# Token rows of keys and values in a hybrid decoder step: 32x32 block transposes on VectorE in place of TensorE transposes

## The chip, the cores and the metric

One Trainium2 chip, one core of it. The metric is the device time of one execution in microseconds, as the median of the runs. A core has TensorE (matmuls, with a weight load beside each), VectorE, ScalarE and GpSimd for the elementwise work, and SP (SyncE), whose queue starts most DMA transfers. In the profile these are PE and PEld, DVE, ACT, POOL and SP.

## What is computed

One inference step of two layers of a decoder. The tokens are 16 meta tokens, 256 prompt tokens and 8 sample sequences of 8 tokens, 336 in all, each 2048 wide. A layer normalizes the tokens and projects them to eight pieces of 2048 columns. Four of these (q, k, v and a gate) feed the retention branch of 8 heads, the others a pooling branch and two gates. The part that matters here:

```
qh = rope(q); kh = rope(k) / 16; vh = v            # per head, 256 wide
scores = einsum('bihd,bjhd->bhij', q, k) * decay
intra  = einsum('bhij,bjhe->bihe', scores, v)
inter  = einsum('bihd,bhde->bihe', q, S) * q_decay
S_new  = S * exp(n * lg) + einsum('bjhd,bjhe->bhde', k * k_decay, v)
```

The prompt starts from an empty state and returns one state of 256x256 a head; each of the 8 sample sequences has its own state S of 256x256 a head, which is read, used and updated. Results are the outputs of both kinds of tokens, the pooling histories and all states.

## The kernel before

**Layout.** Activations are kept transposed: 128 channels in the partitions, tokens along the free dimension, so that a head's keys are one tile of [128, 2, 336] (two halves of 256 channels). All products are taken as three matmuls over a high and a low part of each operand: `hi_of` (L157) rounds on ScalarE to the high part, `lo_of` (L163) subtracts it on VectorE.

**The steps.** The weights of every projection are cut into steps of 512x256 (`steps`, filled by `job`, L89). A step is 24 matmuls (`main_step`, L195), which add up in one of two accumulators in PSUM; four steps make one block of 256 output channels. The main loop (L876) runs over all steps and does in step s, in this program order: the DMA of the weights of step s+4 on SP (`dma_step`), the split of the weights of step s+2 into high (ScalarE, L159) and low (VectorE, L165) parts (`split_step`), the main matmuls of step s, and then the events that are registered for step s. The schedule is written out by hand: each engine runs its instructions in this program order. The split's high and low tiles have four buffers, the raw weights five.

**A head** (`head`, L296) takes 16 steps: 4 for k, 4 for v, 4 for q, 4 for the gate `rg`. `at` (L86) registers a function for a step; in `head` `E(d, fn)` does so relative to the head's first step, and events with d of 16 and more fall into the steps of the next head. `ev_k`, `ev_v`, `ev_q`, `ev_rg` run behind the last step of each block and empty its accumulator; keys and queries are rotated there (`rope`, L301, four VectorE instructions).

**Token rows.** The state updates need keys and values with tokens in the partitions. `tok` (L321) makes them for token blocks of 128, 128 and 80: two TensorE transposes (L328) into a PSUM tile of `side()`, then the high part by ScalarE and the low part by VectorE, with the decay `kd` as scale for keys. This is 12 transposes a head for 16 heads (8 in each of two layers). `stack_out` (L332) writes the rows of block 2, where the sample tokens are, to DRAM on GpSimd's queue; `stack_in` (L338) reads them back on SP's queue in a stacked form: `kttail`, `vttail`, `kts` and `vbd`. With these `sdo(b)` (L425) updates the state of sample sequence b (two matmuls, one VectorE instruction, one DMA out), and `pstate` (L350) makes the prompt's state. `sload(b)` (L411) loads a state into one of 8 buffers on SP's queue; `inter` (L416) reads it before `sdo` updates it in place.

**Around it.** `scores2` (L389, step 14) needs the queries split by `split_q` (step 12); `pv(b)` (L470, steps 17, 19 and 24) multiplies the scores with the value rows and calls `norm`, `norm2` follows a step later, and `back` (L493, step 26) transposes the result on TensorE (L499) for the next projection. In the first head of layer 0 some events are `kl` = 3 steps later, since the norm of the input is not known earlier.

Of the kernel before, what the change touches and what calls it, by code (L numbers as in the profile page):

```python
# [6 lines left out]
F32 = mybir.dt.float32  # L7
F32R = mybir.dt.float32r
# [11 lines left out]
T = NP + NB * NS  # L20
HEADS = 8
HD = 256
# [10 lines left out]
NR0, NR1, NR2 = NP, NP - 128, T - 256  # L33
# [44 lines left out]
def build(tc, a, o, g8):  # L78
    nc = tc.nc
# [6 lines left out]
    def at(s, fn, *args):  # L86
        events[s].append(lambda: fn(*args))
# [15 lines left out]
    def open_pool(name, side=None, **kw):  # L103
        P[name] = tc.alloc_tile_pool(name=name, bufs=1, side=side, reuse_waits="tile", **kw)
        return P[name]
# [4 lines left out]
    def bc(ap, n=2):  # L110
        return ap.unsqueeze(1).to_broadcast([128, n, ap.shape[-1]])
# [9 lines left out]
    def side():  # L121
        return sidep.tile([128, 512], F32, tag="side", bufs=4, name="side")
# [16 lines left out]
    ident = cst[:, C_ID:C_ID + 128]  # L139
# [17 lines left out]
    def hi_of(out, in_, scale=None):  # L157
        if scale is None:
            nc.scalar.copy(out=out, in_=in_)  # L159
        else:  # L160
            nc.scalar.activation(out=out, in_=in_, func=ACTF.Copy, scale=scale)  # L161

    def lo_of(out, in_, hi, scale=None):  # L163
        if scale is None:
            nc.vector.tensor_tensor(out=out, in0=in_, in1=hi.bitcast(F32), op=ALU.subtract)  # L165
        else:
            nc.vector.scalar_tensor_tensor(out=out, in0=in_, scalar=scale, in1=hi.bitcast(F32),  # L167
                                           op0=ALU.mult, op1=ALU.subtract)
# [92 lines left out]
    H = {}  # L261

    for l in range(DEPTH):
# [10 lines left out]
        def z_of(acc, tile_, n):  # L274
            nc.vector.tensor_tensor(out=tile_[:, :, n], in0=acc[:, :, n], in1=bc(rstd[:, n]), op=ALU.mult)

        def open_r(l=l, a_side=a_side):
            p = open_pool("r", side=a_side)
            t = p.tile([128, 2, 8, 32], F32, name="qpad")
            nc.gpsimd.memset(t, 0.0)  # L280
            H["qpad"] = t
            t = p.tile([128, SC], F32, name="sc")
            nc.gpsimd.memset(t[64:128, NR0 + NR1:SC], 0.0)
            H["sc"] = t
            t = p.tile([128, 2, 4, HD], F32R, name="vbd")
            nc.gpsimd.memset(t.bitcast(F32), 0.0)
            H["vbd"] = t
            for key in ("kt", "vt"):
                t = p.tile([128, HD], F32R, name=key + "tail")
                nc.gpsimd.memset(t[64:128].bitcast(F32), 0.0)  # L290
                H[key + "tail"] = t

        def tmp():
            return P["r"].tile([128, 2, T], F32, tag="tmp", bufs=6, name="tmp")

        def head(h, l=l, c0=c0, n=n, nt=nt):  # L296
            hs = {}
            rp = lambda shape, dt, tag, bufs=1: P["r"].tile(shape, dt, tag=tag, bufs=bufs, name=tag)
            kd = lambda b, rows=128: cst[0:rows, C_KD + 3 * h + b:C_KD + 3 * h + b + 1]

            def rope(acc, out, n):  # L301
                t1, t2 = tmp(), tmp()
                nc.vector.tensor_tensor(out=t1[:, :, n], in0=acc[:, :, n], in1=bc(cosr[:, n]), op=ALU.mult)
                nc.vector.tensor_tensor(out=t2[:, :, n], in0=acc[:, :, n], in1=bc(sinr[:, n]), op=ALU.mult)
                nc.vector.tensor_tensor(out=out[:, 0, n], in0=t1[:, 0, n], in1=t2[:, 1, n], op=ALU.subtract)
                nc.vector.tensor_tensor(out=out[:, 1, n], in0=t1[:, 1, n], in1=t2[:, 0, n], op=ALU.add)

            def ev_k(acc):
                hs["kr"] = tmp()
                rope(acc, hs["kr"], slice(0, T))  # L310

            def split_k():
                hs["khi"], hs["klo"] = rp([128, 2, T], F32R, "khi"), rp([128, 2, T], F32R, "klo")
                hi_of(hs["khi"], hs["kr"])
                lo_of(hs["klo"], hs["kr"], hs["khi"])

            def ev_v(acc):
                hs["vr"] = tmp()
                z_of(acc, hs["vr"], slice(0, T))

            def tok(src, b, key, scale):  # L321
                rows = (128, 128, NR2)[b]
                if b == 2:
                    hs[key] = rp([128, 3, HD], F32R, key + "hi"), rp([128, 3, HD], F32R, key + "lo")
                hi, lo = hs[key]
                ps = side()
                for d in range(2):
                    nc.tensor.transpose(ps[:rows, 128 * d:128 * d + 128], hs[src][:, d, 128 * b:128 * b + rows], ident)  # L328
                hi_of(hi[:rows, b], ps[:rows, :HD], scale)
                lo_of(lo[:rows, b], ps[:rows, :HD], hi[:rows, b], scale)  # L330

            def stack_out(key):  # L332
                hs[key + "d"] = tc.dram_tile([NR2 // 8, 4, 8, HD], F32, name=key + "d")
# [159 lines left out]
            def back():  # L493
                ac = tmp()
                on = hs["on"]
                for d in range(2):
                    ps = side()
                    for b, (r0, rows) in enumerate(((c0, 128 - c0), (128, 128), (256, NR2))):
# [5 lines left out]
                                    in_=ac[:, :, n])  # L504

            b0, e = job(wblk(w_in, OFF["k"] + HD * h), 4, h_rhs, 0, ev_k, 3 if l == 0 and h == 0 else 0)
            job(wblk(w_in, OFF["v"] + HD * h), 4, h_rhs, 0, ev_v)
            job(wblk(w_in, OFF["q"] + HD * h), 4, h_rhs, c0, ev_q)
            job(wblk(w_in, OFF["rg"] + HD * h), 4, h_rhs, c0, ev_rg)
            E = lambda d, fn, *ar: at(b0 + d, lambda: fn(*ar))  # L510
            kl = 3 if l == 0 and h == 0 else 0
            E(4 + kl, split_k)
            E(6 + kl, tok, "kr", 2, "kt", kd(2, NR2))
            E(6 + kl, tok, "kr", 0, "kt", kd(0))
            E(7 + kl, tok, "kr", 1, "kt", kd(1))
            E(7 + kl, stack_out, "kt")
            E(9 + kl, stack_in, "kt")
            E(9 + kl, tok, "vr", 2, "vt", None)
            E(9 + kl, tok, "vr", 0, "vt", None)
            E(10 + kl, tok, "vr", 1, "vt", None)  # L520
            E(10 + kl, stack_out, "vt")
            E(12 + kl, stack_in, "vt")
            E(12, split_q)
            E(16, pstate)
            E(11, scores)
            E(14, scores2)
            for b in range(NB):
                E(6 + b, sload, b)
            E(15, inter)
            for b in range(NB):  # L530
                E(15 + b, sdo, b)
            E(16, inter_copy)
            E(17, pv, 0)
            E(18, norm2, 0)
# [8 lines left out]
        if l == 0:  # L543
            at(6, open_r)
        else:
            at(r0 - 1, open_r)
        for h in range(HEADS):
            head(h)
# [357 lines left out]
    parts = (xsq, H["sq_last"][:, 0], H["sq_last"][:, 1])  # L906
# [73 lines left out]
```

## Time and profile before

| What | Value |
|---|---|
| median of 3 runs | 2835.64 us (2835.21 to 2836.82) |
| the profiled execution | 2836.14 us |
| its span in the trace | 2834.4 us |
| mean granted TensorE clock | 0.997 of full speed |
| busy: TensorE, VectorE, ScalarE, GpSimd | 99%, 53%, 33%, 12% |
| moved by DMA | 516.64 MB, mean 182 GB/s |

A row of the profile names a line of the kernel (L328), an engine, an operation, the tiles out<-in, a shape as partitions x elements, and how often it occurs. Busy times are in us, means of one instruction in ns. In the timelines and the chain each row begins with its start in us from the start of the span and its length in us. The chain that ended last is followed back from the last instruction of the execution; time that an engine has in the chain is time on the path. Matmuls overlap, so the time of one in the chain is shorter than its listed duration.

### The profile page before, as it was taken

To read this page: it belongs to the slowest core of one execution; us is meant where nothing else is said; L and a number is where in the kernel's file an instruction comes from. 1 tells how busy PE (TensorE), PEld (TensorE's weight loads), DVE (VectorE), ACT (ScalarE), POOL (GpSimd) and SP (SyncE) were. 2 spreads that over 40 slices of the span, in tenths; PEclk is the share of its full clock that TensorE was granted. 3 is DMA by queue.
4 is the path that set the end of the run, shared out by engine and by line. 5 is a ranking of instruction groups with operands and counts; after the bars stand their busy time and mean duration, and the time that the engine had idled before them with its cause. 6 is when DMAs were issued, how large, how long until landed. Compare 5 with 4: busy or idle time off the path is not lost.

```text
span 2834.4 us, 46399 instructions
## 1 busy us (share of the span) xinstructions
PE 2819.7 (99%) x19234; PEld 2796.5 (99%) x19234; DVE 1509.9 (53%) x1906; ACT 936.2 (33%) x1121; POOL 341.3 (12%) x543
## 2 busy tenths in 40 slices
PE   9999999999999999999999999999999999999998
PEld 9999999999999999999999999999999999999998
DVE  6555555554345664345456666555544455644543
ACT  5333333334233333233333333333342333333333
POOL 1222222210000000000112222222100000000001
PEclk9999999999999999999999999999999999999998
DMA  7566565654544444444555666666555544444443
GB/s 262 208 211 208 208 206 195 227 188 165 164 161 153 147 147 136 152 173 167 180 184 209 211 211 211 216 219 215 205 168 176 171 153 160 142 158 163 172 162 129
DMA packets 174260, 516.64 MB, mean 182 GB/s; under 512 B 23888, under 2 KB 46672, under 8 KB 174032
## 3 DMA queue, kind: packets, MB, share of 16 engines
q1 hardware_dynamic: 151264, 448.37, 46.4%
q0 software_dynamic: 21696, 63.99, 6.4%
q8 instruction: 151, 2.47, 0.4%
q10 hardware_dynamic: 1088, 1.31, 0.1%
q14 instruction: 61, 0.50, 0.1%
HBM read 447.91 MB, written 66.57 MB: 182 GB/s over the span
## 4 chain that ended last, share of the span: by engine, by line
PE 99%; DVE 0%; DMA 0%; issue 0%; POOL 0%; SPq 0%; DVEq 0%; ACT 0%; ACTq 0%
PE acc L155 93%; PE side L155 6%; PE side L328 1%; PE side L499 0%; DMA raw<-in_w_in_dram 0%; DVE xf L922 0%; PE side L252 0%; POOL trs L913 0%; DVE whi L190 0%; DVEq L968 0%; DVE h_lo L167 0%; DVE xs L794 0%; ACT sq L799 0%; DVE wlo L165 0%; SPq L841 0%
## 5 line engine op out<-in xcount | busy, mean ns | idle before, releaser
L155 PE MATMUL acc<-act_hi,whi 128*128 128x320 f32 (+1 forms) x3328 | 1039.6, 312 | 0.0
L155 PE MATMUL acc<-act_lo,whi 128*128 128x320 f32 (+1 forms) x3328 | 1037.3, 312 | 0.0
L155 PE MATMUL acc<-act_hi,wlo 128*128 128x320 f32 (+1 forms) x3328 | 1036.2, 311 | 0.0
L165 DVE TENSOR_TENSOR wlo<-raw,whi 128x1024 fp32r<-128x1024 f32 (+1 forms) x721 | 865.5, 1220 | 293.3 <-ACT whi L159 285.4
L159 ACT CAST whi<-raw 128x1024 fp32r<-128x1024 f32 x719 | 733.8, 1049 | 499.6 <-PE acc L155 394.9
L155 PE MATMUL acc<-h_hi,whi 128*128 128x336 f32 x2304 | 731.6, 319 | 0.0
L155 PE MATMUL acc<-h_lo,whi 128*128 128x336 f32 x2304 | 727.6, 317 | 0.9 <-DVE h_lo L167 0.9
L155 PE MATMUL acc<-h_hi,wlo 128*128 128x336 f32 x2304 | 725.8, 317 | 0.0
L155 PEld LDWEIGHTS acc<-act_lo,whi 128*128 128x128 f32 x3328 | 626.5, 188 | 0.0
L155 PEld LDWEIGHTS acc<-act_hi,wlo 128*128 128x128 f32 x3328 | 625.1, 188 | 0.0
L155 PEld LDWEIGHTS acc<-act_hi,whi 128*128 128x128 f32 x3328 | 624.9, 188 | 0.0
L155 PEld LDWEIGHTS acc<-h_lo,whi 128*128 128x128 f32 x2304 | 435.3, 189 | 1.4 <-DVE h_lo L167 1.4
L155 PEld LDWEIGHTS acc<-h_hi,wlo 128*128 128x128 f32 x2304 | 432.8, 188 | 0.0
L155 PEld LDWEIGHTS acc<-h_hi,whi 128*128 128x128 f32 x2304 | 432.3, 188 | 0.3 <-issue 0.3
L432 DVE SCALAR_TENSOR_TENSOR sraw<-sraw,side 128x512 f32<-128x512 f32 x128 | 87.9, 687 | 175.4 <-PE side L155 175.4
L433 POOL DMA_DIRECT2D out_ret_s_dram<-sraw x128 | 71.6, 560 | 524.1 <-DVE sraw L432 518.0
L226 POOL TENSOR_TENSOR xsq<-sq 128x336 f32<-128x336 f32 (+1 forms) x2 | 1.8, 894 | 564.8 <-ACT sq L222 564.8
L161 ACT ACTIVATE kthi<-side,cst 128x256 fp32r<-128x256 f32 (+1 forms) x48 | 21.0, 470 | 136.4 <-PE side L328 136.4
L159 ACT CAST vthi<-side 128x256 fp32r<-128x256 f32 (+1 forms) x48 | 16.2, 372 | 146.1 <-PE side L328 146.1
L683 POOL DMA_DIRECT2D out_pool_u_dram<-uc x16 | 8.8, 547 | 440.4 <-DVE uc L638 440.4
L596 DVE SCALAR_TENSOR_TENSOR mb<-tr,acc 128x336 f32<-128x336 f32 (+1 forms) x32 | 14.4, 493 | 81.0 <-PE acc L155 81.0
L403 DVE TENSOR_TENSOR sc<-side,dtab 128x416 f32<-128x416 f32 (+1 forms) x16 | 9.3, 583 | 90.3 <-PE side L155 90.3
(165 smaller groups left out, 1844.0 us busy)
## 6 DMA issues: line engine op xcount, KB each, us to landing
raw<-in_w_in_dram SPq DMA_DIRECT2D x512, 512.0 KB, 4.3
sraw<-in_state_ret_dram SPq DMA_DIRECT2D x128, 256.0 KB, 4.2
out_ret_s_dram<-sraw POOLq DMA_DIRECT2D x128, 256.0 KB, 2.6
raw<-in_proj_ret_dram SPq DMA_DIRECT2D x64, 512.0 KB, 4.3
raw<-in_proj_pool_dram SPq DMA_DIRECT2D x64, 512.0 KB, 5.3
raw<-in_w_out_dram SPq DMA_DIRECT2D x64, 512.0 KB, 5.1
raw<-in_pool_w_dram SPq DMA_DIRECT2D x16, 512.0 KB, 3.3
kts<-ktd SPq DMA_DIRECT2D x16, 256.0 KB, 3.0
```

Of the source, the lines that this page charges most:

```text
L155: nc.tensor.matmul(out, lhsT, rhs, start=start, stop=stop)
L159: nc.scalar.copy(out=out, in_=in_)
L161: nc.scalar.activation(out=out, in_=in_, func=ACTF.Copy, scale=scale)
L165: nc.vector.tensor_tensor(out=out, in0=in_, in1=hi.bitcast(F32), op=ALU.subtract)
L226: eng.tensor_tensor(out=xsq[:, n], in0=sq[:, 0, n], in1=sq[:, 1, n], op=ALU.add)
L328: nc.tensor.transpose(ps[:rows, 128 * d:128 * d + 128], hs[src][:, d, 128 * b:128 * b + rows], ident)
L403: nc.vector.tensor_tensor(out=sc[:, w], in0=ps[:, w], in1=dtab[:, w], op=ALU.mult)
L432: nc.vector.scalar_tensor_tensor(out=s2, in0=s2, scalar=g8[h], in1=up, op0=ALU.mult, op1=ALU.add)
L433: nc.gpsimd.dma_start(out=o["ret_s"][l, b, h].rearrange("p (d e) -> p d e", d=2), in_=s)
L596: nc.vector.scalar_tensor_tensor(out=t[:, d, n], in0=H["tr", l, i][:, d, n], scalar=1.0, in1=acc[:, d, n], op0=ALU.add, op1=ALU.mult)
L683: nc.gpsimd.dma_start(out=o["pool_u"][l, 2 * g + i], in_=gs.pop(("uc", i)))
```

## The change

Keys and values are kept in fixed tiles of [128, 2, 384], `kr` and `vr`, whose columns behind the 336 tokens are zero. `turn` copies a tile to token rows in 32x32 blocks: for a group of 32 channels (`a_`, four of them) and a group `t` of 32 tokens in each block of 128, one VectorE transpose reads 32 partitions and writes 32 other partitions of a tile `tok` in SBUF; it covers both halves of the channels and all token blocks at once, 192 elements a partition (128 for t = 3, where block 2 has no tokens). Each event of `turn` has four of these instructions; keys have them in steps 5 to 8, values in steps 9 to 12. `tok` now takes its high and low parts from that tile. The steps of `tok`, `stack_out` and `stack_in` move, and `pstate` and `sdo` come two steps later.

```diff
--- before.py
+++ after.py
@@ -279,6 +279,10 @@
             t = p.tile([128, 2, 8, 32], F32, name="qpad")
             nc.gpsimd.memset(t, 0.0)
             H["qpad"] = t
+            for key in ("kr", "vr"):
+                t = p.tile([128, 2, 384], F32, name=key)
+                nc.gpsimd.memset(t[:, :, T:384], 0.0)
+                H[key] = t
             t = p.tile([128, SC], F32, name="sc")
             nc.gpsimd.memset(t[64:128, NR0 + NR1:SC], 0.0)
             H["sc"] = t
@@ -306,28 +310,36 @@
                 nc.vector.tensor_tensor(out=out[:, 1, n], in0=t1[:, 1, n], in1=t2[:, 0, n], op=ALU.add)
 
             def ev_k(acc):
-                hs["kr"] = tmp()
-                rope(acc, hs["kr"], slice(0, T))
+                rope(acc, H["kr"], slice(0, T))
 
             def split_k():
                 hs["khi"], hs["klo"] = rp([128, 2, T], F32R, "khi"), rp([128, 2, T], F32R, "klo")
-                hi_of(hs["khi"], hs["kr"])
-                lo_of(hs["klo"], hs["kr"], hs["khi"])
+                kr = H["kr"][:, :, 0:T]
+                hi_of(hs["khi"], kr)
+                lo_of(hs["klo"], kr, hs["khi"])
 
             def ev_v(acc):
-                hs["vr"] = tmp()
-                z_of(acc, hs["vr"], slice(0, T))
-
-            def tok(src, b, key, scale):
+                z_of(acc, H["vr"], slice(0, T))
+
+            def turn(key, parts):
+                src = H[key + "r"].rearrange("p d (b t i) -> p d b t i", b=3, t=4)
+                if 0 in parts:
+                    hs[key + "tok"] = rp([128, 3, HD], F32, "tok", 2)
+                dst = hs[key + "tok"].rearrange("p b (d a k) -> p d b a k", d=2, a=4)
+                for a_ in parts:
+                    q = slice(32 * a_, 32 * a_ + 32)
+                    for t in range(4):
+                        nb = 3 if t < 3 else 2
+                        nc.vector.transpose(dst[32 * t:32 * t + 32, :, 0:nb, a_], src[q, :, 0:nb, t])
+
+            def tok(b, key, scale):
                 rows = (128, 128, NR2)[b]
                 if b == 2:
-                    hs[key] = rp([128, 3, HD], F32R, key + "hi"), rp([128, 3, HD], F32R, key + "lo")
-                hi, lo = hs[key]
-                ps = side()
-                for d in range(2):
-                    nc.tensor.transpose(ps[:rows, 128 * d:128 * d + 128], hs[src][:, d, 128 * b:128 * b + rows], ident)
-                hi_of(hi[:rows, b], ps[:rows, :HD], scale)
-                lo_of(lo[:rows, b], ps[:rows, :HD], hi[:rows, b], scale)
+                    hs[key + "t"] = rp([128, 3, HD], F32R, key + "thi"), rp([128, 3, HD], F32R, key + "tlo")
+                hi, lo = hs[key + "t"]
+                raw = hs[key + "tok"][:rows, b]
+                hi_of(hi[:rows, b], raw, scale)
+                lo_of(lo[:rows, b], raw, hi[:rows, b], scale)
 
             def stack_out(key):
                 hs[key + "d"] = tc.dram_tile([NR2 // 8, 4, 8, HD], F32, name=key + "d")
@@ -510,25 +522,28 @@
             E = lambda d, fn, *ar: at(b0 + d, lambda: fn(*ar))
             kl = 3 if l == 0 and h == 0 else 0
             E(4 + kl, split_k)
-            E(6 + kl, tok, "kr", 2, "kt", kd(2, NR2))
-            E(6 + kl, tok, "kr", 0, "kt", kd(0))
-            E(7 + kl, tok, "kr", 1, "kt", kd(1))
-            E(7 + kl, stack_out, "kt")
-            E(9 + kl, stack_in, "kt")
-            E(9 + kl, tok, "vr", 2, "vt", None)
-            E(9 + kl, tok, "vr", 0, "vt", None)
-            E(10 + kl, tok, "vr", 1, "vt", None)
-            E(10 + kl, stack_out, "vt")
-            E(12 + kl, stack_in, "vt")
+            for i in range(4):
+                E(5 + i + kl, turn, "k", (i,))
+                E(min(9 + i + kl, 12), turn, "v", (i,))
+            E(9 + kl, tok, 2, "k", kd(2, NR2))
+            E(9 + kl, stack_out, "kt")
+            E(9 + kl, tok, 0, "k", kd(0))
+            E(10 + kl, tok, 1, "k", kd(1))
+            E(11 + kl, stack_in, "kt")
+            E(13, tok, 2, "v", None)
+            E(13, stack_out, "vt")
+            E(13, tok, 0, "v", None)
+            E(14, tok, 1, "v", None)
+            E(15, stack_in, "vt")
             E(12, split_q)
-            E(16, pstate)
+            E(18, pstate)
             E(11, scores)
             E(14, scores2)
             for b in range(NB):
                 E(6 + b, sload, b)
             E(15, inter)
             for b in range(NB):
-                E(15 + b, sdo, b)
+                E(17 + b, sdo, b)
             E(16, inter_copy)
             E(17, pv, 0)
             E(18, norm2, 0)
```

## Rows read from the trace of the kernel before

**Rows 1.** The page, part 1: busy us (share of the span) xinstructions.

```profile
PE 2819.7 (99%) x19234; PEld 2796.5 (99%) x19234; DVE 1509.9 (53%) x1906; ACT 936.2 (33%) x1121; POOL 341.3 (12%) x543
```

**Rows 2.** TensorE's waits, first and last of four; us in total, times, longest.

```profile
PE side L252 <- DVE sinr L250: 1.5, 1, 1.5
...
PE side L155 <- ACT sq L799: 0.6, 1, 0.6
```

**Rows 3.** The chain that ended last: start us, us, what; L328's pieces.

```profile
46.25 0.44 PE side L328 x4
50.40 0.22 PE side L328 x2
...
66.14 1.78 PE side L155 x18
...
1968.93 0.22 PE side L328 x2
```

**Rows 4.** Line L328, the matmuls alone; duration in ns min/median/max.

```profile
L328 PE MATMUL side<-cst,tmp x192: 270/272/274, 46.1 to 1968.9; 128*128 128x128 f32 x128, 128*80 128x128 f32 x64
```

**Rows 5.** VectorE's groups by form; busy us, mean ns, idle before.

```profile
L165 DVE TENSOR_TENSOR wlo<-raw,whi 128x1024 fp32r<-128x1024 f32 x719 | 864.2, 1222 | 293.3 <-ACT whi L159 285.4
L432 DVE SCALAR_TENSOR_TENSOR sraw<-sraw,side 128x512 f32<-128x512 f32 x128 | 87.9, 687 | 175.4 <-PE side L155 175.4
...
L638 DVE TENSOR_TENSOR uc<-acc,rstd 128x158 f32<-128x158 f32 x16 | 5.2, 323 | 68.6 <-PE acc L155 68.6
...
L642 DVE TENSOR_TENSOR ext<-acc,rstd 128x64 f32<-128x64 f32 x32 | 5.7, 220 | 0.5
```

**Rows 6.** Busy time in one head; columns PE, PEld, DVE, ACT, POOL.

```profile
190.00:261.00 71.00, 71.00 (x504) 69.66 (x503) 41.66 (x59) 21.45 (x29) 17.48 (x28) 1.00 0.63 217
```

**Rows 7.** VectorE's timeline, first head and fourth head: start us, us, what.

```profile
54.37 0.86 DVE L303 TENSOR_TENSOR tmp<-acc,cosr 128x672 f32<-128x672 f32 x1 [1.05 <-PE acc L155]
...
56.88 1.23 DVE L165 TENSOR_TENSOR wlo<-raw,whi 128x1024 fp32r<-128x1024 f32 x1
...
59.64 0.86 DVE L165 TENSOR_TENSOR qlo<-tmp,qhi 128x672 fp32r<-128x672 f32 x1 [0.18 <-ACT qhi L159]
...
247.31 0.87 DVE L167 SCALAR_TENSOR_TENSOR ktlo<-side,cst,kthi 80x256 fp32r<-80x256 f32 x2
...
255.96 0.43 DVE L459 BATCH_NORM_STATS2 bs<-side 80x6 f32<-80x256 f32 x1 [2.32 <-PE side L155]
256.42 0.18 DVE L460 BATCH_NORM_AGGREGATE mv<-bs 80x2 f32<-80x6 f32 x1
...
258.44 0.54 DVE L467 TENSOR_SCALAR on<-side,mv,rs 80x256 f32<-80x256 f32 x1 [0.72 <-POOL rs L462]
...
264.11 1.04 DVE L501 SCALAR_TENSOR_TENSOR tmp<-side,vec,sg 128x336 f32<-128x336 f32 x2 [1.38 <-PE side L499]
```

**Rows 8.** The chain again, steps 11 to 14 of a head in either layer.

```profile
192.68 0.58 PE side L499 x6
...
193.48 14.87 PE acc L155 x96
...
1760.93 14.03 PE acc L155 x96
```

**Rows 9.** DMA issues by line: times, KB each, us to landing.

```profile
raw<-in_w_in_dram SPq DMA_DIRECT2D x512, 512.0 KB, 4.3
...
vbd<-vtd SPq DMA_DIRECT2D x64, 64.0 KB, 2.0
...
vtd<-vtlo POOLq DMA_DIRECT2D x32, 80.0 KB, 2.6
```

**Rows 10.** Timelines of GpSimd and of SP's queue, issues of stacked values.

```profile
195.53 0.57 POOL L336 DMA_DIRECT2D vtd<-vtlo  x1
...
199.64 2.04 SPq L348 DMA_DIRECT2D vbd<-vtd  x4
```

**Rows 11.** Waits of SP's queue at L340: us in total, times, longest.

```profile
SPq L340 <- DMA vtd<-vtlo: 162.8, 17, 14.3
```

## The prediction, written before the changed kernel ran

> **What bounds the kernel now.** I read the busy shares first: TensorE 99%, VectorE 53%, ScalarE 33% [rows 1]. A busy share of 99% could still hide stalls, so the second view is TensorE's own waits: four in the whole span, from 1.5 us down to 0.6 us, all at the start or the end [rows 2]. TensorE never waits between them. So time is removed only by taking work off TensorE, and added only where the change makes TensorE wait. The third view, the chain that ended last, shows how much of the path the touched line L328 is: 64 pieces, 32 of 0.44 us (four transposes) and 32 of 0.22 us (two) [rows 3]. The transpose itself is listed with 272 ns [rows 4], but these overlap; the chain gives 0.11 us each, and that is the price to use.
>
> **Removed from TensorE.** 12 transposes per head, 16 heads: 32 x (0.44 + 0.22) = 21.1 us, all on the path [rows 3].
>
> On the price of one transpose the chain says 0.11 us. [...]
>
> **Added to VectorE.** Per head 32 block transposes, eight events of four: three of 32 partitions x 192 elements, one of 32 x 128. The trace has no such instruction. Nearest rows by size: 64 elements 220 ns, 158 elements 323 ns [rows 5]. The slope is 103/94 = 1.10 ns an element and the fixed part 150 ns, so 192 elements cost 360 ns and 128 elements 290 ns. An event U is then 3 x 0.36 + 0.29 = 1.37 us, and a head 8 x 1.37 = 11.0 us. Bounds: from below 0.22 us an instruction (the 64-element row; a gain is excluded, since these are added to an engine that saves nothing), from above 1.22 us (the 1024-element row) [rows 5]. [...]
>
> In a stretch of 71 us, one head, VectorE is busy for 41.7 us and ScalarE for 21.4 us [rows 6]. With 11.0 us more VectorE stands at 52.7 of 69.7 us. The mean leaves room; what decides is the densest stretch, where the split of the next weights (L165, `wlo`, 1.22 us a step) stands in VectorE's queue behind the new work and must end before the step that reads it, two steps on.
>
> **The densest stretch, steps 8 to 14 of a head.** VectorE last waits for TensorE at the head's step 8 (`pv(2)` of the head before). From there, up to the split for step 14, it has: norm 0.61, U, split 1.23, `norm2` 0.54, U, two key lows 0.87, split 1.23, `back` 1.04, U, another key low 0.44 (half of a pair), split 1.23, `rope` of q 2.51, U, split 1.23 [rows 7]: 10.9 us + 4U. TensorE has five main steps and the transposes of `back` in the same time: four steps take 14.87 us in layer 0 and 14.03 us in layer 1, `back` 0.58 [rows 8], so 19.2 us and 18.1 us. The splits are in time while U is under 2.07 us in layer 0 and 1.80 us in layer 1. At U = 1.37 the VectorE sum is 16.4 us; it even waits again for the end of step 11 before `rope` of q. From there the split ends after 2.51 + 1.37 + 1.23 = 5.1 us, and TensorE takes 7.4 us (7.0 in layer 1) over two steps: about 2 us to spare. No stall in 15 of 16 heads.
>
> **The first head of layer 0** differs: keys are turned in steps 8 to 11 and all four value events fall on step 12. `rope` of q begins at 54.37 us [rows 7], 0.66 us earlier without the first two pieces of [rows 3], so at 53.7; then 2.51 + U + 1.23 + 4U + 0.87 + 0.86 (`qlo`) has the queries split at 59.2 + 5U = 66.0 us [rows 3, 7]. The scores stand on TensorE at 66.14 us [rows 3], now 1.32 us earlier, at 64.8. TensorE waits 1.2 us, once. Had the block transposes overlapped like the other VectorE rows (pitch some 0.09 us under the duration), this would vanish.
>
> [...]
>
> **Moved.** `stack_out`, `stack_in`, the state updates `sdo` and `pstate` go two to four steps later. At U = 1.37 the value lows of block 2 end 1.5 us into step 14. Four issues on GpSimd at about 0.6 us, 2.6 us to land, then on SP `vttail` and four `vbd` issues at 0.5 us each, and 2.0 us to land [rows 9, 10]: 11 us after the start of step 14. `sdo(0)`, now behind step 17, is due after four steps of 3.72 us, the scores (1.78) [rows 3] and `inter`: 16.7 us without `inter`. Margin 5.7 us or more. Had `sdo` stayed behind step 15 it would be due at 9.2 us plus `inter`, about when the values land; so the delay buys the margin. Queued behind the waiting `stack_in` on SP are the weight loads of later steps. SP already waits there for 162.8 us in 17 waits without TensorE waiting once [rows 2, 11]; raw weights land in 4.3 us [rows 9] and are asked for four steps ahead. I take nothing. The state buffers come free two steps later, so `sload` of the next head may wait on SP for `out_ret_s`; the same lead covers it. On GpSimd, `stack_out` now stands behind the `qpad` copies; it is inside the 1.5 us above or its margin.
>
> **Edits costed at nothing.** ScalarE's and VectorE's hi/lo of the turned rows read SBUF instead of PSUM: ScalarE is idle 70% of a head, and its waits for L328 go; for VectorE the rows above were used (bounds 0 to 0.1 us each, inside the 2 us). Four more memsets on GpSimd at the start of a layer and a larger pool: a wait of 0 to 2 us there, I take 0, because what they fill is not read before two steps have passed. TensorE's four side buffers are asked for six times less per head.
>
> **Sum.** The profiled execution took 2836.1 us (span 2834.4); 2836.1 - 21.1 + 1.2 = 2816.2. The median of the runs is 0.5 us below that execution, so 2815.7 us.
>
> **The rivals.**
> *VectorE at half rate, no change.* If every element costs double in a block transpose (150 ns + 192 x 2.2 = 571 ns; 431 ns for 128), U is 2.14 us. The stretch overruns by 0.28 us in layer 0 and 1.36 us in layer 1: 8 x 0.28 + 8 x 1.36 = 13.1 us, and the first head 5.1 us: 18.2 us given back, 2832.7 us. [...] Against it: every single-pass row of VectorE goes by one element in 1.1 ns. [...]
>
> *VectorE becomes the bound, slower.* Above U = 2.07 us every head pays; the time given back is 69U - 129.5 us (64U of the sixteen heads and 5U of the first, less the room worked out above), which passes 21.1 us at U = 2.18 us, an instruction of about 0.58 us. With the 0.69 us of the 512-element row [rows 5], U is 2.57, 47.8 us come back, and the time is 2862 us. The place is TensorE waiting for `wlo` at steps 13 to 15 of every head. [...]
>
> *A wait for the stacked values takes the place.* If `vbd` lands over 5.7 us later than worked out, TensorE waits at `sdo(0)`; each further us costs 16 us, so 1.3 us more returns the whole gain, at 2836 us. Against it: the margin is a step and a half.
>
> **How the numbers follow.** About 0.2%, 5.7 us, can be told from no change. Forecast, with U up to 1.9 us: 0.80. Half rate: 0.08, mostly no change. VectorE as the bound: 0.08. The wait for stacked values: 0.04, split over the three signs. That gives faster 0.84, same 0.07, slower 0.09. The range starts below the full 21.1 us without any stall (2814.5, less 2 us of scatter) and reaches up to U = 1.95 us (first head 4.1 us, layer 1 about 5 us: some 2824) and a small unforeseen wait: 2812 to 2826.
>
> **What would show it.** Right: no L328 on TensorE, its waits still a handful with one of 1 to 2 us around 66 us, VectorE some 175 us busier (512 instructions near 0.36 us), `sdo` not waiting for `vbd`. Wrong: TensorE waits for `wlo` L165 in every head (VectorE price), or for DMA `vbd` (margin), or block transposes far from 0.36 us.

## The result and the profile after

| | before | changed |
|---|---|---|
| median | 2835.72 us (2835.21 to 2836.82) | 2818.61 us (2817.97 to 2822.43) |
| span of the profiled execution | 2834.4 us | 2816.9 us |

The ratio is 0.9942, with a 95% interval of 0.993 to 0.9954: the change makes the kernel faster by 17.1 us, 0.6%. The forecast was 2815.7 us, in a range of 2812 to 2826 us.

The first view is again the page's busy times. Against [rows 1] TensorE has 192 instructions less, and VectorE has gone from 53% to 60%, 175 us more:

```profile
PE 2800.1 (99%) x19042; PEld 2778.0 (99%) x19042; DVE 1684.9 (60%) x2418; ACT 940.2 (33%) x1121; POOL 291.9 (10%) x547
```

TensorE's waits stand against [rows 2]: us in total, times, longest. Four are the known ones at the start and the end; the first row is new.

```profile
PE side L155 <- DVE qlo L165: 1.6, 1, 1.6
PE side L252 <- DVE sinr L250: 1.5, 1, 1.5
PE side L155 <- DVE ones L859: 1.1, 1, 1.1
PE acc L155 <- DVE h_lo L167: 1.1, 1, 1.1
PE side L155 <- ACT sq L814: 0.6, 1, 0.6
```

The block transposes, which no row of before showed, are these groups of VectorE (busy us, mean ns, idle before; the values have the same rows):

```profile
L333 DVE STREAM_TRANSPOSE tok<-kr 32x192 f32<-32x192 f32 x192 | 70.7, 368 | 2.9
...
L333 DVE STREAM_TRANSPOSE tok<-kr 32x128 f32<-32x128 f32 x64 | 19.5, 305 | 1.1
```

An event of three and one adds up to 3 x 0.368 + 0.305 = 1.41 us; the prediction had 1.37. In the timeline, with the short gaps between the four, it takes 1.45 us (the row at 199.64 us below), and what follows starts 1.48 us behind its start.

The new wait is in the first head of layer 0, and it costs more than its length. TensorE's timeline there (start us, length us, what), with the scores of step 14 and the main matmuls of step 15:

```profile
64.75 0.29 PE L155 MATMUL side<-qhi,khi 128*128 128x272 f32 x1
66.64 0.39 PE L155 MATMUL side<-qlo,khi 128*128 128x272 f32 x1 [1.60 <-DVE qlo L165]
...
69.52 0.48 PE L155 MATMUL acc<-h_hi,wlo 128*128 128x336 f32 x1
69.80 0.48 PE L155 MATMUL acc<-h_hi,whi 128*128 128x336 f32 x1
...
71.40 0.32 PE L155 MATMUL acc<-h_hi,whi 128*128 128x336 f32 x1
71.56 0.31 PE L155 MATMUL acc<-h_lo,whi 128*128 128x336 f32 x1
```

The second matmul of the scores waits 1.60 us for `qlo`. From then on look at the starts: the main matmuls follow each other every 0.28 us at 69.5 us and every 0.16 us at 71.4 us. The windows of the same stretch show why (columns as in [rows 6], then the granted clock, the DMA share and GB/s):

```profile
60.00:66.00 6.00, 5.03 (x33) 4.79 (x31) 5.78 (x17) 1.88 (x5) 0.29 (x1) 1.00 0.07 21
66.00:70.00 4.00, 3.37 (x21) 3.37 (x22) 4.00 (x7) 0.59 (x2) 3.96 (x4) 0.73 0.16 44
70.00:80.00 10.00, 10.00 (x82) 8.86 (x81) 7.34 (x11) 4.57 (x6) 2.81 (x7) 0.94 0.56 175
```

The granted clock is 0.73 on average from 66 to 70 us and 0.94 from 70 to 80 us. Taken by the single us it is 1.00 from 66 to 67, 0.94 from 67 to 68 and 0.50 in each from 68 to 71 us: matmuls at half clock, right behind the wait. Lost by that: 4 x 0.27 + 10 x 0.06 = 1.7 us. In this execution, the only one of the changed kernel that was traced, the whole event costs 1.6 + 1.7 = 3.3 us.

In all other heads nothing waits. Here is the densest stretch in the third head of layer 0, VectorE's timeline first (answering to [rows 7]), then the chain (to [rows 8]):

```profile
197.03 0.85 DVE L307 TENSOR_TENSOR tmp<-acc,cosr 128x672 f32<-128x672 f32 x1
...
199.64 1.45 DVE L333 STREAM_TRANSPOSE tok<-vr 32x192 f32<-32x192 f32 x4
201.12 1.23 DVE L165 TENSOR_TENSOR wlo<-raw,whi 128x1024 fp32r<-128x1024 f32 x1
```

```profile
193.19 14.91 PE acc L155 x96
```

`rope` of q begins at 197.03 us, the turn at 199.64, the split for step 14 at 201.12 and ends at 202.35. Step 14's matmuls are due three steps into the 14.91 us piece, at about 193.19 + 11.2 = 204.4 us. The split is there 2.0 us early.

How much a head gained is best read from the chain, between the `inter` matmuls of one head and those of the next: before (`inter` and the first `sdo` in one piece of 34), layer 0, then layer 1:

```profile
142.81 2.30 PE side L155 x34
...
213.91 2.30 PE side L155 x34
```

```profile
1710.87 2.30 PE side L155 x34
...
1780.29 2.30 PE side L155 x34
```

and after:

```profile
143.78 1.86 PE side L155 x32
...
213.66 1.86 PE side L155 x32
```

```profile
1699.27 1.86 PE side L155 x32
...
1767.35 1.86 PE side L155 x32
```

Layer 0 went from 71.10 to 69.88 us a head, 1.22 us less; layer 1 from 69.42 to 68.08 us, 1.34 us less. The removed pieces of the chain [rows 3] were worth 1.32 us in each. Over sixteen heads that is 20.5 us; less the 3.3 us of the first head, 17.2 us. The spans differ by 17.5 us, the medians by 17.1 us.

### The profile page after: what moved, and what is told of

It reads as the page before. It is cut to its first block, busy times and chain, and to the rows that moved or that the text cites. A ratio compares the mean times of both kernels' runs of the same rounds, so it can differ in the third digit from the quotient of the medians.

```text
span 2816.9 us, 46574 instructions
## 1 busy us (share of the span) xinstructions
PE 2800.1 (99%) x19042; PEld 2778.0 (99%) x19042; DVE 1684.9 (60%) x2418; ACT 940.2 (33%) x1121; POOL 291.9 (10%) x547
## 4 chain that ended last, share of the span: by engine, by line
PE 99%; DVE 1%; DMA 0%; issue 0%; POOL 0%; SPq 0%; DVEq 0%; ACT 0%; ACTq 0%
PE acc L155 93%; PE side L155 6%; PE side L511 0%; DVE tok L333 0%; DMA raw<-in_w_in_dram 0%; DVE xf L937 0%; DVE wlo L165 0%; PE side L252 0%; POOL trs L928 0%; DVE qlo L165 0%; DVE tmp L307 0%; DVE tmp L308 0%; DVE whi L190 0%; DVEq L983 0%; DVE xs L809 0%
## 5 line engine op out<-in xcount | busy, mean ns | idle before, releaser
L333 DVE STREAM_TRANSPOSE tok<-vr 32x192 f32<-32x192 f32 (+1 forms) x256 | 90.3, 353 | 4.3
L333 DVE STREAM_TRANSPOSE tok<-kr 32x192 f32<-32x192 f32 (+1 forms) x256 | 90.3, 353 | 4.1
L775 DVE SCALAR_TENSOR_TENSOR mt<-tp,acc 128x336 f32<-128x336 f32 (+1 forms) x32 | 14.4, 492 | 80.4 <-PE acc L155 80.4
L809 DVE SCALAR_TENSOR_TENSOR xs<-acc,xo 128x672 f32<-128x672 f32 (+2 forms) x17 | 13.5, 800 | 80.5 <-PE acc L155 80.5
L275 DVE TENSOR_TENSOR tp<-acc,rstd 128x672 f32<-128x672 f32 (+1 forms) x16 | 13.5, 841 | 80.4 <-PE acc L155 80.4
```

The costliest lines, as they stand in the source:

```text
L333: nc.vector.transpose(dst[32 * t:32 * t + 32, :, 0:nb, a_], src[q, :, 0:nb, t])
L775: nc.vector.scalar_tensor_tensor(out=t[:, d, n], in0=H["tp", l, i][:, d, n], scalar=1.0, in1=acc[:, d, n], op0=ALU.add, op1=ALU.mult)
L809: nc.vector.scalar_tensor_tensor(out=xs[:, p, n], in0=acc[:, p, n], scalar=0.5, in1=xo[:, p, n], op0=ALU.mult, op1=ALU.add)
```

## The experiments

The theory: VectorE's new work is hidden in fifteen heads, the removed transposes are worth their time in the chain, and what is missing to the full gain is the first head's wait with the slow matmuls behind it. The rival: a small cost in every head.

**The first head's turns spread out (e1_spread).**

```diff
-                E(5 + i + kl, turn, "k", (i,))
-                E(min(9 + i + kl, 12), turn, "v", (i,))
+                E(8 + i // 2 if kl else 5 + i, turn, "k", (i,))
+                E(10 + i // 2 if kl else 9 + i, turn, "v", (i,))
```

> The changed kernel, with the first head's turns alone moved: keys in steps 8 and 9, values in steps 10 and 11, two events each, none on step 12. Theory: the changed kernel misses the full 21.1 us by 3.3 us that all lie in the first head, 1.6 us of TensorE's wait for qlo and 1.7 us of matmuls at half the granted clock behind it. Then both go: some 2815.3 us, no TensorE wait for qlo, granted clock 1.00 between 66 and 80 us. Rival: the missing us are spread over all heads (VectorE's extra work in each): then the time stays within 1 us of the changed kernel's 2818.6 us.

Measured: 2816.76 us (2816.54 to 2816.90), ratio 0.9932 (0.9919 to 0.9944). The wait for `qlo` is gone and the granted clock is 1.00 from 66 to 80 us. One wait is new, in the steps into which the turns were put:

```profile
PE acc L155 <- DVE wlo L165: 0.5, 1, 0.5
```

In the first head 2.9 us came back (the first `inter` matmuls start 2.9 us earlier), which is 3.3 less 0.5; the other heads have the same period. The theory stands as to the place, and the rival (within 1 us of 2818.6 us) does not; but this edit moved the load and made a smaller wait of it. The time is 1.5 us above the 2815.3 us of the theory: in the total, 1.9 us came back; of the span 0.6 us were lost again behind the last head, where the kernels are the same.

**No block transposes at all (e4_no_turn).** All turns are left out; the token rows are taken from a constant tile:

```diff
-                E(5 + i + kl, turn, "k", (i,))
-                E(min(9 + i + kl, 12), turn, "v", (i,))
...
-                raw = hs[key + "tok"][:rows, b]
+                raw = H["tok"][:rows, b]
```

> The changed kernel without any block transpose: the token rows of keys and values are read from a constant tile, so the turning is left out of the computation. Theory: in 15 of 16 heads the turns are hidden, so this saves only what moving them in the first head saves: 2814.5 to 2815.5 us, equal to the kernel with the first head's turns moved. Rival: turns cost something in every head: this is 2 us or more below that kernel.

Measured: 2815.76 us (2815.20 to 2815.95), ratio 0.9928 (0.9915 to 0.9940), 1.0 us below the spread kernel, of which 0.5 us is that kernel's wait for `wlo`. The periods of the heads are 69.89 and 68.08 us with and without the transposes. The time is 0.3 us above the range of the theory and well short of the rival's 2 us. So VectorE's new work, 175 us in all, is hidden completely in fifteen heads, and another order of the turns could bring at most the 2.9 us by which this kernel is below the changed one.

**One value event of the first head earlier (e7_v0_at_10), and the same with a longer last event (e11_short_wait).**

```diff
-                E(min(9 + i + kl, 12), turn, "v", (i,))
+                E(min(9 + i + kl, 12) - (2 if kl and i == 0 else 0), turn, "v", (i,))
```

> The changed kernel, with one of the first head's four value events moved from step 12 to step 10, 1.4 us of VectorE earlier. Theory: the wait for qlo shrinks from 1.6 to about 0.2 us and the granted clock does not fall behind so short a wait: 2815.5 us. Rival: the clock falls there for another reason than the wait: the wait shrinks, but the matmuls between 68 and 71 us stay at half clock: 2817.2 us.

Measured: 2816.77 us (2815.99 to 2817.05), ratio 0.9931 (0.9916 to 0.9946). The time lies between the theory's 2815.5 us and the rival's 2817.2 us, nearer to the rival, but the trace speaks for the theory: the wait is 0.3 us and no matmul between 60 and 80 us runs at half clock:

```profile
PE side L155 <- DVE qlo L165: 0.3, 1, 0.3
```

The first head's `inter` matmuls start 3.2 us earlier than in the changed kernel (70.58 us against 73.82); 1.0 us of that is lost again behind the last head, where the kernels are the same.

The second kernel makes two transposes of that head's last value event twice:

```diff
+                    for t in (0, 1, 2, 3) if not first or key != "v" or a_ != 3 else (0, 0, 1, 1, 2, 3):
```

> The changed kernel with one value event of the first head at step 10 (TensorE waits 0.3 us for qlo there), and two block transposes of that head's last value event done twice, which makes the wait about 1.1 us. If the granted clock falls behind a wait of that length as behind 1.6 us: 2819.2 us. If it stays: 2817.5 us.

Measured: 2817.32 us (2817.09 to 2817.66), ratio 0.9934 (0.9920 to 0.9947). TensorE's wait and the windows around it:

```profile
PE side L155 <- DVE qlo L165: 1.1, 1, 1.1
```

```profile
64.00:68.00 4.00, 2.92 (x25) 2.68 (x24) 3.97 (x9) 1.70 (x4) 3.14 (x4) 1.00 0.15 41
68.00:72.00 4.00, 4.00 (x35) 3.57 (x37) 3.05 (x6) 1.56 (x2) 3.91 (x7) 1.00 0.67 222
```

The wait of 1.1 us costs its length, and the granted clock stays at 1.00. In the trace of the changed kernel it fell at this place, behind 1.6 us. None of the traces with a shorter wait there or none (this one, e7_v0_at_10, e1_spread, e4_no_turn, and two below) has half clock in the first head. So the slow matmuls go with the wait. That its length alone decides is not shown: the next experiment but one has 1.6 us of waiting at the same place, and there the clock stays.

**The moves alone (e2_moves_only).** The kernel before, TensorE transposes kept, all steps as in the change:

```diff
-            E(6 + kl, tok, "kr", 2, "kt", kd(2, NR2))
...
+            E(9 + kl, tok, "kr", 2, "kt", kd(2, NR2))
...
-            E(16, pstate)
+            E(18, pstate)
...
-                E(15 + b, sdo, b)
+                E(17 + b, sdo, b)
```

> The kernel before, TensorE transposes kept, with only the steps of the change: token rows, stacking and state updates at the steps that the change gives them. Theory: the moves are free, 2835.7 us, the gain comes from the removed transposes alone. Rival: the moves bring part of the gain or cost part of it: over 2 us away from 2835.7 us.

Measured: 2836.25 us (2835.64 to 2839.38), ratio 1.0003 (0.9994 to 1.0012). In the total the moves neither bring nor cost anything that can be measured; the gain is the removed transposes. By its trace a head takes 71.16 us in layer 0 (`inter` at 142.62 and 213.78 us) and 69.35 us in layer 1 (at 1710.88 and 1780.23 us): the moves add 0.06 us a head in layer 0 and take 0.07 us away in layer 1, and against this kernel the removed transposes are worth 1.28 and 1.27 us a head.

**The updates not delayed (e3_sdo_15).**

```diff
-            E(18, pstate)
+            E(16, pstate)
...
-                E(17 + b, sdo, b)
+                E(15 + b, sdo, b)
```

> The changed kernel with the updates not delayed: sdo from step 15 and pstate at step 16, as before the change, all else changed. Theory: the stacked values land some 11 us after the start of step 14 and sdo(0) is due at about the same time, so TensorE waits for vbd by 0 to 2 us in most heads and by some 4 us in the first, and the clock may fall behind the longer waits: 2822 to 2850 us. Rival: the margin is larger than worked out and the delay was not needed: 2818.6 us.

Measured: 2821.70 us (2820.18 to 2823.01), ratio 0.9950 (0.9933 to 0.9966). TensorE waits once for the values, in the first head, and the other fifteen heads do not wait at all:

```profile
PE side L155 <- DMA vbd<-vtd: 3.6, 1, 3.6
```

The chain in front of that wait (start us, us, what):

```profile
64.55 0.49 DVE ktlo L167
65.32 1.12 POOL ktd L348 x2
...
66.48 2.84 POOL qpad L393 x2
...
70.23 1.62 POOL vtd L348 x3
71.85 2.75 DMA vtd<-vtlo
...
75.33 2.06 DMA vbd<-vtd
...
77.43 0.50 PE side L155 x2
```

Read it downwards: the key low comes late, since all value events of that head stand ahead of it; GpSimd issues the keys' transfers, then copies `qpad` for 2.84 us, and only then the values' transfers; their landing, SP's `vbd` loads and `sdo(0)` follow. The wait of 3.6 us is again followed by a lower granted clock: 0.87 on average from 76 to 80 us and 0.70 from 80 to 84, 1.7 us lost. Half of the theory holds: the delay is needed, but by one head only, and the time is just below the theory's 2822 us.

This trace has the changed kernel's wait for `qlo` too, as long and at the same place (it ends at 66.24 us), and here the granted clock stays at 1.00 behind it:

```profile
PE side L155 <- DVE qlo L165: 1.6, 1, 1.6
```

```profile
64.00:68.00 4.00, 2.40 (x23) 2.16 (x21) 3.94 (x9) 2.00 (x4) 2.63 (x4) 1.00 0.15 41
68.00:72.00 4.00, 4.00 (x31) 3.79 (x33) 3.18 (x7) 1.46 (x2) 4.00 (x7) 1.00 0.56 162
```

So one and the same wait was followed by half clock in one execution and not in another: its length alone does not decide.

**The values' transposes twice (e5_v_twice), all of them twice (e6_all_twice), and six for four (e9_six_for_four).** These measure the price of VectorE's work when it no longer fits. Some transposes are repeated; the three new lines belong to the three kernels in this order:

```diff
-                    for t in range(4):
+                    for t in (0, 1, 2, 3) * (2 if key == "v" else 1):
...
+                    for t in (0, 1, 2, 3) * 2:
...
+                    for t in (0, 0, 1, 1, 2, 3):
```

> The changed kernel with every block transpose of the values done twice (an event of 2.8 us in steps 9 to 12, keys as they are). By the working of the prediction the split for step 14 is late by 1.6 us in layer 0 and 2.7 us in layer 1, and the first head's queries by some 7 us: 40 us of waits, 2855 us. Theory with the clock: each wait of 1.6 us or more is followed by matmuls at half clock for about as much again, some 27 us more: 2882 us. Rival: VectorE has more room than worked out: under 2825 us.

Measured: 2876.74 us, one execution, between the two theories. The waits are 45.9 us where 40 were worked out; an event takes 3.03 us in the timeline instead of 2.8:

```profile
PE acc L155 <- DVE wlo L165: 34.7, 15, 2.8
PE side L155 <- DVE qlo L165: 11.2, 13, 7.8
```

The clock theory fails: it had half clock behind every wait of 1.6 us or more, some 27 us. The granted clock fell behind the first head's wait of 7.8 us (0.53 from 68 to 79 us) and behind three of the fifteen waits for `wlo` (those that end at 288.7, 507.3 and 1587.3 us, with 0.74, 0.57 and 0.70 in the lowest window of 4 us); behind the other twelve, of 1.5 to 2.8 us, it stayed at 1.00. That is some 10 us lost. About 5 us of the time were not traced to anything.

> The changed kernel with every block transpose done twice, keys and values (an event of 2.8 us). The prediction's 69U - 129.5 us gives 65 us of waits: 2880 us; with the clock at half behind each wait, some 2907 us. Rival: the transposes still fit, under 2830 us.

Measured: 2953.67 us, one execution. Here the working fails: 97.2 us of waits instead of 65, and `back` waits for `on` too. With 8 x 3.03 us a head VectorE no longer catches up before step 8, where the working lets the stretch begin: in the third head it last waits for TensorE at 191.87 us, ahead of the first key event of step 5.

```profile
PE acc L155 <- DVE wlo L165: 70.7, 46, 2.9
PE side L511 <- DVE on L479: 14.7, 14, 1.4
PE side L155 <- DVE qlo L165: 11.8, 7, 9.8
```

> The changed kernel with six block transposes in each event instead of four (two of them done twice), an event of 2.2 us, near the 2.14 us of the prediction's half-rate rival, which gives 2833 us. By the same working with 2.24 us: 25 us of waits, 2840 us. With the clock at half behind each wait of over a microsecond, which the prediction left out: 2845 to 2860 us. Rival: VectorE has more room, under 2825 us.

Measured: 2858.52 us (2858.23 to 2860.51), ratio 1.0080 (1.0066 to 1.0094): slower than before. The waits are 26.9 us; the prediction's 69U - 129.5 us gives 25 us for U = 2.24:

```profile
PE acc L155 <- DVE wlo L165: 21.3, 15, 2.1
PE side L155 <- DVE qlo L165: 5.6, 1, 5.6
```

But the time is 43 us above 2815.3 us, where the changed kernel would be without its first head's stall. A lower clock behind the waits makes up most of the rest: 5 us behind the first head's 5.6 us (granted clock 0.57 from 70 to 82 us), 2 us near the start (0.57 from 9 to 13 us), and some 8 us in layer 1 (five stretches, with 0.57 to 0.71 in the lowest window of 4 us). From the second head of layer 1 on every head has the same wait of about 2.0 us. Here is the wait as it stands for the second and for the third, and then a window of 30 us for each:

```profile
PE acc L155 <- DVE wlo L165: 2.0, 1, 2.0
```

```profile
1570.00:1600.00 30.00, 27.95 (x214) 26.57 (x213) 20.57 (x38) 10.95 (x16) 5.89 (x13) 1.00 0.63 221
1640.00:1670.00 30.00, 27.95 (x204) 26.58 (x203) 19.89 (x35) 9.26 (x13) 5.09 (x11) 0.94 0.65 228
```

The head in the first window takes 70.40 us, the one in the second 71.94 us: 1.54 us more for the same wait, with a mean granted clock of 0.94. Of seven heads with this wait, five took about 71.94 us. So a wait of this length often, not always, costs nearly double.

**A version that beats both (e8_split_q_first, e10_delay_first_only).** One value event of the first head at step 10 and, in that head alone, `split_q` ahead of the turns of step 12; then also the delay of the updates in that head alone:

```diff
+            if kl:
+                E(12, split_q)
...
-                E(min(9 + i + kl, 12), turn, "v", (i,))
+                E(min(9 + i + kl, 12) - (2 if kl and i == 0 else 0), turn, "v", (i,))
...
-            E(18, pstate)
+            E(18 if kl else 16, pstate)
...
-                E(17 + b, sdo, b)
+                E((17 if kl else 15) + b, sdo, b)
```

> The kernel with one value event of the first head at step 10, and in that head the split of the queries placed ahead of the value events of step 12 too. Theory: the last 0.3 us of TensorE's wait for qlo go, and the split for step 15 still ends in time: 2816.3 us, no wait of TensorE between 35 and 2790 us. Rival: the split for step 15 becomes late instead, TensorE waits for wlo, 2817 us or more.

Measured: 2816.24 us (2815.83 to 2818.03), ratio 0.9931 (0.9918 to 0.9943). TensorE waits only at the start and the end.

> The same, and state updates delayed by two steps in the first head alone: in the other 15 heads sdo from step 15 and pstate at step 16, as before the change. Theory: in those heads the values land about 1 us before sdo(0) is due, so the delay does nothing there: the time of the kernel without this edit, within 0.5 us. Rival: 1 us is too little in some heads; TensorE waits for vbd again, 2818 us or more.

Measured: 2815.41 us (2815.04 to 2815.71), ratio 0.9927 (0.9913 to 0.9940), with no wait for `vbd`. It is 0.8 us below the kernel without this edit, where at most 0.5 us was expected; a head takes 0.02 us less by the traces, 0.4 us in all, and the rest was not traced. It is 3.2 us below the changed kernel and the fastest of those that compute everything; its runs lie wholly below those of the changed kernel, but the intervals of the ratios overlap. Whether the delay can go in the first head too, now that the keys are ready earlier there, was not tried.

## Why the prediction was right, and where it was off

**What bounds the kernel** held: TensorE is at 99% in both, and the time followed what came off it and what it had to wait for.

**Removed**: 21.1 us were predicted. The periods show 1.22 us a head in layer 0 and 1.34 us in layer 1 instead of 1.32 us: 20.5 us. The price from the chain was right to 3%. The difference between the layers comes from the moves: against e2_moves_only, which has them too, the transposes are worth 1.28 and 1.27 us.

**Added**: 0.36 us for 192 elements and 0.29 us for 128 were taken from the slope of two unrelated rows; measured 0.368 and 0.305 us. The half-rate rival is out. Consecutive transposes of 192 elements mostly start 0.38 us apart, no less than their duration, while the first two instructions of `rope`, 0.85 us each, start 0.77 us apart (197.03 and 197.80 us in the third head). That full durations have to be counted was the author's estimate, which no row of before shows; the runs bear it out, and the sum was even a little short: the gaps make an event 1.45 us long instead of 1.41. Why the block transposes do not overlap as those rows do, no run here shows. 64 elements more cost 63 ns, 0.98 ns an element, against 1.10 ns between the rows of [rows 5].

**The densest stretch** held: about 2 us to spare were worked out for the split of step 14, 2.0 us were there. Six for four bears the working out: 25 us of waits worked out, 26.9 measured.

**The first head** is the term that was mis-sized. The place and the cause (`qlo` behind the turns of step 12) were right; the wait was put at 1.2 us and measured 1.6. That comes from the size of an event: the prediction's 59.2 + 5U has `qlo` ready at 66.0 us for U = 1.37, and at 66.6 us for the 1.48 us from one event's start to the next instruction; it was ready at 66.58 us. What the working put at nothing is that TensorE may not come back at full speed: a granted clock of 0.50 from 68 to 71 us followed in the traced execution and cost 1.7 us, so the term measured 3.3 us there. This is 2.1 of the 2.9 us by which the forecast missed; the 0.6 us of the removed part are the next. How much half clock the three other executions behind the median had was not traced, and e3_sdo_15 had the same wait without any.

**The rivals.** VectorE as the bound exists where it was put, at `wlo` in step 14, but its price was too low. Half rate was priced at 2833 us, no change; six for four, with an event hardly longer (2.24 us against 2.14), measured 2858.5 us, clearly slower. Again the working of the waits was right, and the clock behind them was missing. By the prediction's formula an event of 2.24 us gives back 25 us, 4 us more than the gain; measured, it costs 23 us more than before. So the break-even probably lies below the 2.18 us of the prediction; where it lies was not measured.

**Moved.** Free, as predicted: in the control (e2_moves_only) as a whole, and without a wait in fifteen heads. The values land with `vbd` issued until 212.43 us plus 2.0 us [rows 9], at 214.4 us, 10 us after the start of step 14; the prediction said 11:

```profile
207.63 0.57 POOL L348 DMA_DIRECT2D vtd<-vtlo  x1
```

```profile
210.44 1.99 SPq L360 DMA_DIRECT2D vbd<-vtd  x4
```

The first `sdo` two steps earlier would be due behind `inter`, which starts at 213.66 us and takes 1.86 us, at 215.5 us. So 1.1 us of margin were there where the prediction saw none, and the delay of two steps bought something in the first head only.

## What to carry to other kernels

When one engine is on the path for 99% of the time, work may be moved off it at a bad exchange rate (here 11.3 us of VectorE for 1.3 us of TensorE), as long as the queue it moves into has room in its densest stretch; work that out step by step against the due times, because the mean share of 60% says nothing of it. Look at the irregular iteration separately: the first head alone, with its events pushed together, cost 3.3 of some 20 us. And price a wait of TensorE twice, at its length and with the 1.5 to 1.7 us that a lower clock behind it cost here: of the waits of 1.5 to 3.6 us some were followed by that and others of the same length were not.

## What was not expected

**The price of a wait.** Waits of 0.3, 0.5 and 1.1 us in the first head, and of 0.9 us in later heads (e9_six_for_four), left the granted clock at 1.00. A wait of 1.6 us was followed by matmuls at half clock (0.50) in the changed kernel and not in e3_sdo_15 (1.00), at the same place. A wait of 3.6 us (e3_sdo_15) was followed by 0.87 and 0.70 over 4 us each, for 1.7 us lost as behind the 1.6 us; waits of 2.0 us were followed by a lower clock in five of seven heads of e9_six_for_four (0.57 to 0.71 in the lowest window of 4 us), and waits of 1.5 to 2.8 us in three of the fifteen cases of e5_v_twice (0.57 to 0.74). Nor is 1.1 us safe everywhere: in e9_six_for_four the clock of 0.57 from 9 to 13 us stands behind two waits of 0.7 and 1.1 us. What decides was not found; it is not the length of the wait alone.

**ScalarE took longer from SBUF than from PSUM.** The high parts of the token rows were costed at nothing. Before and after (min/median/max ns):

```profile
L161 ACT ACTIVATE kthi<-side,cst x48: 458/473/478, 46.5 to 1956.1; 128x256 fp32r<-128x256 f32 x32, 80x256 fp32r<-80x256 f32 x16
```

```profile
L161 ACT ACTIVATE kthi<-tok,cst x48: 493/503/514, 57.6 to 1948.3; 128x256 fp32r<-128x256 f32 x32, 80x256 fp32r<-80x256 f32 x16
```

The key instruction went from 473 to 503 ns with only its source moved from PSUM to SBUF, the one for values from 372 to 406 ns; without any block transposes (e4_no_turn) they take 502 and 401 ns, so the transposes are not the reason. VectorE's key lows, of whose two tensor operands one made the same move, took 476 ns before and 481 after. Neither is on the path.
